# First branch's projection of two token blocks moved into and behind the last attention head; w_out loaded by column halves

## The chip, the cores and the metric

One core of one Trainium2 chip runs the kernel. Its engines work beside each other, each on its own list of instructions in a fixed order: TensorE (PE, matrix multiplications and transposes; PEld is its weight load), VectorE (DVE), ScalarE (ACT), GpSimd (POOL) and SyncE (SP, which here issues most loads and stores; POOL and ACT issue some). The metric is the device time of one execution, in microseconds (us).

## The reference

One layer of a decoder with two token mixers, 2048 tokens, width 1024, all float32:

```python
h = rms_norm(x, norm_mix)
q, c_kv, k_rope, q_idx, k_idx, w_idx, uv, gates = split(h @ w_in)
y_a = dsa_mixer(...)                  # 8 heads; 256 keys per query, chosen by an indexer
y_b = chunked_gmlp(uv, ...)           # u * (W_s LN(v) + b), chunks of 128
g_a, g_b = split(sigmoid(gates))
merged = g_a * (y_a @ w_proj_a) + g_b * (y_b @ w_proj_b)
x = x + merged @ w_out
h = rms_norm(x, norm_ffn)
x = x + (silu(h @ w_gate) * (h @ w_up)) @ w_down
return rms_norm(x, final_norm)
```

The change touches the line `merged` and the load of `w_out`. `y_a` and `y_b` are 2048 x 512, both projections 512 x 1024.

## The kernel before, in words

A float32 product is made of three passes: every operand is split into a part h that the fast float format holds and a remainder l (`split`, L148 to L157: a copy, then a subtraction), and `mm3` (L159 to L163) adds h·h, h·l and l·h. So one 512-token column block of a projection with 4 weight tiles is 12 matrix instructions.

The work runs in stages: input projections and the choice of keys; attention over 8 heads (L901 to L937); the merge and `w_out` with the residual (called stage 3 here, L940 to L1112); the two feed-forward products by a seven-product scheme; the down projection and the final norm.

**Attention.** For head h and each of four blocks j of 512 queries, `s_stage` makes scores (PE), adds the mask (DVE, tile Pt, L818) and takes exponentials (ACT, L824); `v_stage` transposes the probabilities (tile ptp, L835), splits them (pth, ptl) and multiplies by the values (tile O, L842 and L843), and at its end turns the result (pto, L855) and stores it to `d_ya` (L859). A loop over the 32 blocks interleaves `v_stage` of a block with `s_stage` of the next. Into every block it also puts some units of a filler generator, as many as the table `FILL` says for j = 0 to 3. The filler is `project_b`: for each 512 tokens, four units that turn 128 columns of `y_b` (`branch_T`, tile pty, four transposes each) and eight units that project (`project`, tile ppr, 12 matrix instructions, L161 to L163), multiply by the gate (DVE, tile sg, L887) and store to `d_mb`. That is 48 units, 6 for each of the 8 heads.

**Stage 3.** For each j of four 512-token blocks: `y_a` of the block is turned (`a_T`), then for m = 0 to 7 the projection of `y_a` is made (`project`), added to `d_mb` (POOL, tile mb, L1072) and split (mgh, mgl); then for m = 0 to 7 the product with `w_out` (tile po, 24 matrix instructions, all eight mgh and mgl as operands), the residual and the squares. At j = 0 the sixteen half rows of `w_out` are loaded and split in the same loop over m (tile wor, L1082, into woh and wol). The block before's norm is finished by `stats` (pss, pbc) and, from j = 2 on, `prep_b` readies the next stage's operands. `branch_T` and `project` have in stage 3 a pool of their own (`pr`) with 4 buffers for loads, 4 for sg and 3 for each half of a split weight; in attention the pool `fill` has 2 of each.

**What sets the order.** The kernel is written once as a sequence and a scheduler puts it into each engine's list; a buffer that is used again waits for its last reader. SP's list is in order too: a load that waits for a buffer holds back all behind it. On-chip memory is given out as a stack from the left and one from the right; a tile of stage 3 waits for the attention tile that lies at its address.

Of the kernel before, what the change touches and what calls it, by code (L numbers as in the profile page):

```python
# [11 lines left out]
F32 = mybir.dt.float32  # L12
F32R = mybir.dt.float32r
# [4 lines left out]
ALU = mybir.AluOpType  # L18
# [3 lines left out]
P = 128  # L22
S = 2048
# [3 lines left out]
H = 8  # L27
# [12 lines left out]

FILL = (1, 1, 2, 2)

# [17 lines left out]
def block_kernel(ctx, tc, xT, xN, pos, g_mix, w_in, g_kv, w_ukT, w_uvT, ln_g, ln_b, w_sT, b_sT,  # L60
# [704 lines left out]


    c2 = ExitStack()
    mp, _ = open_pool("mp", stack=c2)
    aw, _ = open_pool("aw", 2, stack=c2)
    fl_, _ = open_pool("fill", stack=c2)  # L770
    masks = []
# [89 lines left out]

    def branch_T(pl, src, j, tag, bk, nb):

        yh = pl.tile([P, 4, 512], F32R, name="yth", tag="yh" + tag, bufs=1)
        yl = pl.tile([P, 4, 512], F32R, name="ytl", tag="yl" + tag, bufs=1)
        for c in range(4):
            yt = pl.tile([P, 4, P], F32, name="ytk", tag="fin", bufs=nb)
            sp.dma_start(yt, src[j * 512:(j + 1) * 512, c * P:(c + 1) * P].rearrange("(t p) c -> p t c", p=P))
            pt = bank(bk, "pty")
            for t in range(4):  # L870
                pe.transpose(pt[:, t * P:(t + 1) * P], yt[:, t], ident)
            split(yh[:, c, :], yl[:, c, :], pt, dve)
            yield yh, yl

    def project(pl, w_p, m, y, s, rows, bk, nb):

        wh = pl.tile([P, 4, P], F32R, name="wph", tag="wph", bufs=2 + nb // 4)
        wl = pl.tile([P, 4, P], F32R, name="wpl", tag="wpl", bufs=2 + nb // 4)
        raw = pl.tile([P, 4, P], F32, name="wpr", tag="fin", bufs=nb)
        sp.dma_start(raw, w_p[m])  # L880
        split(wh, wl, raw, pool, hi=pool)
        pm = bank(bk, "ppr")
        for k in range(4):
            mm3(pm, wh[:, k, :], wl[:, k, :], y[0][:, k, :], y[1][:, k, :], k == 0, k == 3)
        sg = pl.tile([P, 512], F32, name="sg", tag="sg", bufs=nb)
        sp.dma_start(sg, d_sg[s * D + m * P:s * D + (m + 1) * P, rows])
        dve.scalar_tensor_tensor(sg, sg, 1.0, pm, op0=ALU.add, op1=ALU.mult)  # L887
        return sg

    def project_b():  # L890

        for j in range(4):
            rows = slice(j * 512, (j + 1) * 512)
            for yb in branch_T(fl_, d_yb, j, "b", "C", 2):
                yield
            for m in range(KT):
                sg = project(fl_, w_pb, m, yb, 1, rows, "C", 2)
                pool.dma_start(d_mb[m * P:(m + 1) * P, rows], sg)
                yield

    def interleave(gens):  # L901
# [19 lines left out]
    for n, (h, j) in enumerate(blocks):  # L921
# [137 lines left out]
    sp.dma_start(gf, g_ffn)  # L1059
    sp.dma_start(gl, g_fin)  # L1060
    for j in range(4):
        rows = slice(j * 512, (j + 1) * 512)
        if j == 0:
            ya = a_T(0)
        mh, ml = [], []
        for m in range(KT):
            mb = pw.tile([P, 512], F32, name="mb", tag="mb", bufs=4)
            sp.dma_start(mb, d_mb[m * P:(m + 1) * P, rows])
            sg = project(pr_, w_pa, m, ya, 0, rows, "A", 4)
            if after and m == 1:  # L1070
# [7 lines left out]
            if j == 0:
                for n in range(2):
                    ns = slice(n * 512, (n + 1) * 512)  # L1080
                    raw = pw.tile([P, 512], F32, name="wor", tag="xo", bufs=4)
                    sp.dma_start(raw, w_out[m * P:(m + 1) * P, ns])  # L1082
                    split(woh[m][:, ns], wol[m][:, ns], raw, dve, 0.5)
# [287 lines left out]
```

## Time and profile before

| what | value |
|---|---|
| time, median of 3 runs (lowest to highest) | 3208.24 us (3203.16 to 3210.06) |
| the profiled execution's own time | 3207.25 us |
| its span in the trace | 3205.5 us |
| PE busy | 3061.6 us, 96% |
| DVE, ACT, POOL busy | 71%, 45%, 39% |
| attention's last instruction on PE (last pto) | 1598.5 us after the start |

In the trace's rows an instruction is given with its line, engine, operation and tiles (out<-in); in brackets stands the engine's idle time just before it and what ended it. "PEclk" is the share of full speed that TensorE's clock was granted, a mean over the stretch: it has two levels, 1.2 and 2.4 GHz (0.5 and 1.0). At 1.0 a 512-column matrix instruction starts every 0.23 us, though its own duration is printed as 0.39.

### The profile page before, as it was taken

What the parts mean: (1) busy time and instruction counts of PE and PEld (TensorE: products, weight loads), DVE (VectorE), ACT (ScalarE), POOL (GpSimd) and SP (SyncE); (2) the same over time, 40 slices, a digit from 0 to 9 for tenths busy, and PEclk for the clock granted to TensorE, in tenths of its full rate; (3) what the DMA queues carried; (4) which work ended last, traced back from release to release, by engine and by line L of the source; (5) the groups of instructions that cost most, each with busy time, mean ns of one, the idle gap of its engine ahead of it and who ended that gap; (6) DMA issues with size and microseconds to landing.
All of it is one profiled execution on the core that took longest, in us unless ns stands there. A gap on an engine that the chain in (4) does not pass through costs nothing.

```text
span 3205.5 us, 43210 instructions
## 1 busy us (share of the span) xinstructions
PE 3061.6 (96%) x14568; PEld 2516.7 (79%) x14568; DVE 2280.2 (71%) x4150; ACT 1435.1 (45%) x2704; POOL 1255.6 (39%) x1218
## 2 busy tenths in 40 slices
PE   7998999998999999999999999999999999999998
PEld 6876777777778788888777777888878888788887
DVE  8369999999751888877754657777887677544565
ACT  6434435453343767767522125333443333333442
POOL 3644333362454323232253423333345555531220
PEclk9999999999999999999999999999999999999999
DMA  6324333332553222222265853444544444754463
GB/s 204 109 73 138 104 100 102 121 109 81 181 185 125 74 74 78 70 88 69 95 223 168 272 180 122 148 142 150 201 174 173 168 170 158 271 182 141 136 193 106
DMA packets 254416, 453.34 MB, mean 141 GB/s; under 512 B 35568, under 2 KB 79088, under 8 KB 254064
## 3 DMA queue, kind: packets, MB, share of 16 engines
q1 hardware_dynamic: 233840, 390.78, 37.2%
q0 software_dynamic: 15744, 51.39, 4.3%
q10 hardware_dynamic: 4608, 8.39, 0.7%
q8 instruction: 114, 1.87, 0.2%
q14 instruction: 110, 0.90, 0.1%
HBM read 299.54 MB, written 150.93 MB: 141 GB/s over the span
## 4 chain that ended last, share of the span: by engine, by line
PE 67%; DVE 17%; DMA 5%; issue 4%; ACT 3%; POOL 1%; SPq 0%; DVEq 0%; ACTq 0%; POOLq 0%
PE pgu L162 8%; PE pgu L161 7%; PE pgu L163 7%; PE pdn L162 4%; PE pdn L161 4%; PE pdn L163 4%; DVE X L489 4%; PE ptp L835 3%; DVE y L532 3%; PE pm L161 2%; PE pm L162 2%; PE pm L163 2%; PE O L842 2%; PE O L843 2%; PE pg L161 1%
## 5 line engine op out<-in xcount | busy, mean ns | idle before, releaser
L975 POOL TENSOR_TENSOR cmb<-fraw 128x512 f32<-128x512 f32 x275 | 396.7, 1448 | 490.4 <-DVE wfl L154 450.0
L161 PE MATMUL pgu<-fh,wfh 128*128 128x512 f32 x1232 | 480.0, 391 | 7.5 <-ACT fh L153 5.8
L162 PE MATMUL pgu<-fl,wfh 128*128 128x512 f32 x1232 | 481.4, 391 | 2.7 <-DVE fl L154 2.7
L163 PE MATMUL pgu<-fh,wfl 128*128 128x512 f32 x1232 | 481.1, 391 | 0.1
L161 PEld LDWEIGHTS pgu<-fh,wfh 128*128 128x128 f32 x1232 | 232.0, 189 | 58.0 <-ACT fh L153 7.0
L162 PEld LDWEIGHTS pgu<-fl,wfh 128*128 128x128 f32 x1232 | 232.5, 189 | 52.1 <-DVE fl L154 4.0
L489 DVE SCALAR_TENSOR_TENSOR X<-rl,wi,X 128x512 f32<-128x512 f32 (+3 forms) x266 | 232.3, 883 | 56.5 <-ACT rl L485 43.4
L163 PEld LDWEIGHTS pgu<-fh,wfl 128*128 128x128 f32 x1232 | 232.4, 189 | 49.5 <-DVE wfl L154 1.3
L153 ACT ACTIVATE wfh<-cmb 128x512 fp32r<-128x512 f32 x220 | 138.5, 630 | 261.1 <-POOL cmb L975 133.1
L162 PE MATMUL pdn<-ua,uw 128*128 128x512 f32 (+1 forms) x660 | 247.6, 376 | 2.2 <-DVE ua L154 2.2
L154 DVE TENSOR_TENSOR wfl<-cmb,wfh 128x512 fp32r<-128x512 f32 x220 | 183.8, 843 | 90.0 <-ACT wfh L153 89.4
L154 DVE TENSOR_TENSOR ua<-raw,ua 128x512 fp32r<-128x512 f32 (+1 forms) x165 | 119.6, 729 | 177.7 <-ACT ua L153 177.7
L163 PE MATMUL pdn<-ua,uw 128*128 128x512 f32 (+1 forms) x660 | 245.3, 375 | 0.0
L161 PE MATMUL pdn<-ua,uw 128*128 128x512 f32 (+1 forms) x660 | 239.7, 376 | 1.7 <-ACT ua L153 1.7
L1151 DVE TENSOR_TENSOR s<-s,pgu 128x512 f32<-128x512 f32 x264 | 174.9, 679 | 86.8 <-PE pgu L163 47.8
L161 PE MATMUL pm<-wh,hT 128*128 128x512 f32 (+1 forms) x576 | 221.8, 389 | 13.6 <-ACT zq L413 4.9
L485 ACT ACTIVATE rl<-sc 128x512 f32<-128x512 f32 (+3 forms) x304 | 158.5, 549 | 155.6 <-DVE X L489 87.9
L162 PE MATMUL pm<-wl,hT 128*128 128x512 f32 (+1 forms) x576 | 222.3, 387 | 0.5 <-POOL wl L154 0.4
L163 PE MATMUL pm<-wh,lT 128*128 128x512 f32 (+1 forms) x576 | 221.6, 385 | 0.0
L153 ACT ACTIVATE pth<-ptp 128x512 fp32r<-128x512 f32 (+1 forms) x320 | 162.3, 531 | 121.1 <-PE ptp L835 112.2
L154 POOL TENSOR_TENSOR uw<-raw,uw 128x512 fp32r<-128x512 f32 x77 | 108.4, 1416 | 260.2 <-ACT uw L153 233.9
L154 DVE TENSOR_TENSOR ptl<-ptp,pth 128x512 fp32r<-128x512 f32 (+1 forms) x320 | 185.8, 605 | 30.5 <-ACT pth L153 28.7
(315 smaller groups left out, 7729.1 us busy)
## 6 DMA issues: line engine op xcount, KB each, us to landing
raw<-d_a SPq DMA_DIRECT2D x143, 256.0 KB, 2.7
wraw<-in_w_in_dram SPq DMA_DIRECT2D x64, 512.0 KB, 4.4
d_a<-cmb SPq DMA_DIRECT2D x110, 256.0 KB, 2.3
fraw<-in_w_gate_dram SPq DMA_DIRECT2D x22, 1024.0 KB, 4.9
fraw<-in_w_up_dram SPq DMA_DIRECT2D x22, 1024.0 KB, 5.1
d_sg<-zg POOLq DMA_DIRECT2D x64, 256.0 KB, 2.6
sg<-d_sg SPq DMA_DIRECT2D x64, 256.0 KB, 3.7
d_w<-cmb SPq DMA_DIRECT2D x55, 256.0 KB, 2.1
```

The costliest lines, as they stand in the source:

```text
L153: act.activation(h, src, AF.Copy)
L154: lo.tensor_tensor(l, src, _f(h), op=ALU.subtract)
L161: pe.matmul(out, ah, bh, start=first, stop=False, skip_group_check=onto)
L162: pe.matmul(out, ah, bl, start=False, stop=False, skip_group_check=onto)
L163: pe.matmul(out, al, bh, start=False, stop=last, skip_group_check=onto)
L485: act.activation(r[:, :w], sc[:, :w], AF.Relu)
L489: dve.scalar_tensor_tensor(xs, r[:, :w], wi[:, i, h:h + 1], xs, op0=ALU.mult, op1=ALU.add)
L532: dve.tensor_scalar(y, Xs[p], t[:, p:p + 1], None, op0=ALU.is_ge, op1=ALU.add, accum_out=c[:, p:p + 1])
L835: pe.transpose(pt[:, t * P:(t + 1) * P], out["P"][t, kt // 8][:, (kt % 8) * P:(kt % 8 + 1) * P], ident)
L842: pe.matmul(O[:, cs], V, a[:, cs], start=(kt == 0), stop=False)
L975: eng.tensor_tensor(s, blocks[form[0]], blocks[form[1]], op=form[2])
L1151: dve.tensor_tensor(s[to], s[to], b, op=op)
```

## The change

Four things are done.

1. `FILL` goes from (1, 1, 2, 2) to (1, 2, 2, 2), so that the 48 units of `project_b` are used up in the first seven heads. In the last head nothing is put into block j = 0; blocks 1, 2 and 3 get four units each of the new generator `project_a(0)`: 4 turning units, then 8 projecting units for the first 512 tokens of `y_a`. A projecting unit loads the tile of `d_mb` too (mba), adds on POOL, and stores the merged tile to the new `d_mg`.
2. `project_a(1)` (the next 512 tokens) is written right behind the attention loop, ahead of stage 3's loop.
3. Stage 3 loads j = 0 and 1 from `d_mg` and has no projection there; j = 2 and 3 are as before.
4. `w_out` is loaded ahead of the loop, first the left 512 columns of all 8 rows, then the right.

The pool `fill` is opened below attention's pools and lives until j = 3; it replaces `pr`. It has 3 buffers for loads, 3 for sg and 2 for each half of a split weight. The number of instructions on PE, DVE and ACT is unchanged; POOL and SP get 16 stores and 16 loads more.

```diff
-FILL = (1, 1, 2, 2)
+FILL = (1, 2, 2, 2)
...
+    d_mg = tc.dram_tile([D, S // 2], F32, name="d_mg")
...
+    fl_, c3r = open_pool("fill")
     c2 = ExitStack()
     mp, _ = open_pool("mp", stack=c2)
     aw, _ = open_pool("aw", 2, stack=c2)
-    fl_, _ = open_pool("fill", stack=c2)
...
-    def branch_T(pl, src, j, tag, bk, nb):
+    def branch_T(src, j):
...
-            yt = pl.tile([P, 4, P], F32, name="ytk", tag="fin", bufs=nb)
+            yt = fl_.tile([P, 4, P], F32, name="ytk", tag="fin", bufs=3)
...
-    def project(pl, w_p, m, y, s, rows, bk, nb):
+    def project(w_p, m, y, s, rows, bk):
 
-        wh = pl.tile([P, 4, P], F32R, name="wph", tag="wph", bufs=2 + nb // 4)
-        wl = pl.tile([P, 4, P], F32R, name="wpl", tag="wpl", bufs=2 + nb // 4)
-        raw = pl.tile([P, 4, P], F32, name="wpr", tag="fin", bufs=nb)
+        wh = fl_.tile([P, 4, P], F32R, name="wph", bufs=2)
+        wl = fl_.tile([P, 4, P], F32R, name="wpl", bufs=2)
+        raw = fl_.tile([P, 4, P], F32, name="wpr", tag="fin", bufs=3)
...
+    def project_a(j):
+
+        rows = slice(j * 512, (j + 1) * 512)
+        for ya in branch_T(d_ya, j):
+            yield
+        for m in range(KT):
+            sg = project(w_pa, m, ya, 0, rows, "C")
+            mb = fl_.tile([P, 512], F32, name="mba", tag="fin", bufs=3)
+            sp.dma_start(mb, d_mb[m * P:(m + 1) * P, rows])
+            pool.tensor_tensor(sg, sg, mb, op=ALU.add)
+            pool.dma_start(d_mg[m * P:(m + 1) * P, rows], sg)
+            yield
...
-        gens.append((islice(fill, FILL[j]), FILL[j]))
+        if h + 1 < H:
+            gens.append((islice(fill, FILL[j]), FILL[j]))
+        elif j:
+            gens.append((islice(fill_a, 4), 4))
...
+    for _ in project_a(1):
+        pass
+    for n in range(2):
+        ns = slice(n * 512, (n + 1) * 512)
+        for k in range(KT):
+            raw = pw.tile([P, 512], F32, name="wor", tag="xo", bufs=4)
+            sp.dma_start(raw, w_out[k * P:(k + 1) * P, ns])
+            split(woh[k][:, ns], wol[k][:, ns], raw, dve, 0.5)
     for j in range(4):
...
-            sp.dma_start(mb, d_mb[m * P:(m + 1) * P, rows])
-            sg = project(pr_, w_pa, m, ya, 0, rows, "A", 4)
+            sp.dma_start(mb, (d_mg if j < 2 else d_mb)[m * P:(m + 1) * P, rows])
+            if j > 1:
+                sg = project(w_pa, m, ya, 0, rows, "A")
+                pool.tensor_tensor(mb, mb, sg, op=ALU.add)
```

How the change moves instructions is shown at three places (in the changed kernel the same statements stand one line lower up to L164 and thereabouts, and some 10 lower in stage 3).

**PE, from the last head's block j = 2 into block j = 3** (S: scores; ptp: turned probabilities; ppr: filler). Before:

```order
L814 MATMUL S<-Kst_9189,qah 128x512
L815 MATMUL S<-Kst_9189,qal 128x512
L855 MATMUL pto<-ident,os 128x128 x4
L814 MATMUL S<-Kst_9189,qah 128x512
L815 MATMUL S<-Kst_9189,qal 128x512
L814 MATMUL S<-Kst_9189,qah 128x512
L815 MATMUL S<-Kst_9189,qal 128x512
L835 MATMUL ptp<-ident,Pt 128x128 x6
L842 MATMUL O<-pth,V 128x512
L161 MATMUL ppr<-yth,wph 128x512
```

The change:

```order
L162 MATMUL ppr<-yth,wph 128x512
L163 MATMUL ppr<-ytl,wph 128x512
L164 MATMUL ppr<-yth,wpl 128x512
L815 MATMUL S<-Kst_9190,qah 128x512
L816 MATMUL S<-Kst_9190,qal 128x512
L815 MATMUL S<-Kst_9190,qah 128x512
L816 MATMUL S<-Kst_9190,qal 128x512
L856 MATMUL pto<-ident,os 128x128 x4
L815 MATMUL S<-Kst_9190,qah 128x512
L816 MATMUL S<-Kst_9190,qal 128x512
L836 MATMUL ptp<-ident,Pt 128x128 x3
```

Before, the two projecting units of block j = 2 lie further ahead; now four lie in the block, the last of them just ahead of the block's last scores, so that PE has 24 matrix instructions more between the block's start and the first ptp of the next.

**PE, the end of attention and the start of stage 3** (pty: turned `y_a`; po: product with `w_out`). Before:

```order
L842 MATMUL O<-pth,V 128x128
L843 MATMUL O<-ptl,V 128x128
L855 MATMUL pto<-ident,os 128x128 x4
L871 MATMUL pty<-ident,ytk 128x128 x16
L161 MATMUL ppr<-yth,wph 128x512
L162 MATMUL ppr<-ytl,wph 128x512
```

The change, there and 24 matrix instructions later:

```order
L843 MATMUL O<-pth,V 128x128
L844 MATMUL O<-ptl,V 128x128
L856 MATMUL pto<-ident,os 128x128 x4
L872 MATMUL pty<-ident,ytk 128x128 x16
L162 MATMUL ppr<-yth,wph 128x512
```

```order
L164 MATMUL ppr<-yth,wpl 128x512
L162 MATMUL po<-mgh,woh_18091 128x512 x3
L163 MATMUL po<-mgl,woh_18091 128x512
L164 MATMUL po<-mgh,wol_18099 128x512
L162 MATMUL po<-mgh,woh_18092 128x512
```

The sixteen transposes still stand behind the last pto. Of the block's eight projections two stand ahead of the first po (four before); the other six now lie among the po of j = 0.

**SP, the loads around the same place** (ytk: `y_a`; wpr: projection weights; sg: gates; mb, mba: merged tiles; wor: `w_out`). Before:

```order
L886 DMA sg<-d_sg 128x512 x3
L1068 DMA mb<-d_mb 128x512
L1082 DMA wor<-in_w_out_dram 128x512 x2
L1068 DMA mb<-d_mb 128x512
L1082 DMA wor<-in_w_out_dram 128x512 x2
L1068 DMA mb<-d_mb 128x512 x2
L868 DMA ytk<-d_ya 128x4x128 x4
L886 DMA sg<-d_sg 128x512 x3
L880 DMA wpr<-in_w_pa_dram 128x512
```

The change:

```order
L869 DMA ytk<-d_ya 128x4x128
L887 DMA sg<-d_sg 128x512
L869 DMA ytk<-d_ya 128x4x128
L881 DMA wpr<-in_w_pa_dram 128x512
L909 DMA mba<-d_mb 128x512
L881 DMA wpr<-in_w_pa_dram 128x512
L1080 DMA wor<-in_w_out_dram 128x512 x4
L1087 DMA mb<-d_mg 128x512 x2
L909 DMA mba<-d_mb 128x512
L1087 DMA mb<-d_mg 128x512
L1080 DMA wor<-in_w_out_dram 128x512
```

Before, four loads of `w_out` stand ahead of `y_a`; now all four loads of `y_a` and two of projection weights stand ahead of the first of `w_out`.

## Rows read from the trace of the kernel before

**Rows 1.** The page: span; part 1, busy us (share) xinstructions.

```profile
span 3205.5 us, 43210 instructions
PE 3061.6 (96%) x14568; PEld 2516.7 (79%) x14568; DVE 2280.2 (71%) x4150; ACT 1435.1 (45%) x2704; POOL 1255.6 (39%) x1218
```

**Rows 2.** Windows: attention; stage 3. Length, PE, PEld, DVE, ACT, POOL, PEclk, DMA.

```profile
1040.00:1565.00 525.00, 508.38 (x2986) 426.99 (x2986) 431.84 (x1064) 373.72 (x774) 172.90 (x212) 0.99 0.23 74
1630.00:1906.00 276.00, 266.34 (x1188) 217.22 (x1187) 142.10 (x207) 55.01 (x92) 108.43 (x91) 0.99 0.63 206
```

**Rows 3.** Timeline of PE: start, us; heads 2, 3 and 7, start of j = 3.

```profile
1224.31 0.55 PE L835 MATMUL ptp<-ident,Pt 128*128 128x128 f32 x3 [1.42 <-ACT Pt L824]
1226.06 0.50 PE L842 MATMUL O<-pth,V 128*128 128x512 f32 x1 [1.21 <-ACT pth L153]
1226.39 0.39 PE L161 MATMUL ppr<-yth,wph 128*128 128x512 f32 x1
1226.62 0.39 PE L162 MATMUL ppr<-ytl,wph 128*128 128x512 f32 x1
...
1296.04 0.50 PE L842 MATMUL O<-pth,V 128*128 128x512 f32 x1 [0.96 <-ACT pth L153]
```

**Rows 4.** Windows around the end of attention, columns as in rows 2.

```profile
1570.00:1585.00 15.00, 11.09 (x45) 8.24 (x44) 7.38 (x20) 6.95 (x13) 1.96 (x3) 0.77 0.04 9
...
1600.00:1615.00 15.00, 10.87 (x35) 7.54 (x36) 11.24 (x13) 6.68 (x11) 9.33 (x9) 0.66 0.92 306
1615.00:1630.00 15.00, 12.42 (x47) 9.72 (x46) 12.74 (x15) 5.58 (x9) 11.04 (x9) 0.89 0.80 263
```

**Rows 5.** Waits of PE from 1565 to 1630: us in total, times, longest.

```profile
PE ptp L835 <- ACT Pt L824: 3.2, 1, 3.2
PE po L161 <- ACT mgh L153: 2.6, 1, 2.6
PE ppr L161 <- POOL wph L150: 2.1, 2, 1.1
PE pty L871 <- DMA ytk<-d_ya: 1.7, 2, 1.5
PE pty L871 <- DVE ytl L154: 1.2, 1, 1.2
PE O L842 <- ACT pth L153: 0.7, 1, 0.7
```

**Rows 6.** Timeline of PE: the last pto; the first po.

```profile
1598.49 0.66 PE L855 MATMUL pto<-ident,os 128*128 128x128 f32 x4 [0.69 <-ACT os L846]
...
1622.11 0.73 PE L161 MATMUL po<-mgh,woh 128*128 128x512 f32 x2 [2.58 <-ACT mgh L153]
```

**Rows 7.** Groups of instructions of DVE and POOL, 1600 to 1660: busy us, mean ns.

```profile
L157 DVE SCALAR_TENSOR_TENSOR wol<-wor,woh 128x512 fp32r<-128x512 f32 x16 | 17.3, 1113 | 3.4 <-ACT woh L156 3.3
...
L887 DVE SCALAR_TENSOR_TENSOR sg<-sg,ppr 128x512 f32<-128x512 f32 x9 | 6.1, 682 | 11.7 <-PE ppr L163 11.6
...
L151 POOL TENSOR_TENSOR wpl<-wpr,wph 128x512 fp32r<-128x512 f32 x11 | 15.7, 1433 | 0.1
L1072 POOL TENSOR_TENSOR mb<-mb,sg 128x512 f32<-128x512 f32 x8 | 12.3, 1532 | 6.7 <-DVE sg L887 4.2 <-issue 2.4
L150 POOL CAST wph<-wpr 128x512 fp32r<-128x512 f32 x12 | 9.6, 802 | 14.7 <-PE ppr L162 7.7 <-DMA wpr<-in_w_pa_dram 6.8
```

**Rows 8.** DMA: first stage-3 issue; wor's KB and landing, 1585 to 1630; d_mb's landing.

```profile
1588.50 0.32 SPq L1068 DMA_DIRECT2D mb<-d_mb  x1
...
wor<-in_w_out_dram SPq DMA_DIRECT2D x16, 256.0 KB, 4.8
...
DMA to landing us min/median/max: 2.7/3.2/8.9
```

**Rows 9.** Waits of PE from 1630 to 1900: us in total, times, longest.

```profile
PE po L162 <- DVE mgl L154: 3.3, 2, 2.6
PE pty L871 <- issue: 1.6, 1, 1.6
```

More of the change, by code (lines that the diff above doesn't have):

```diff
@@ L860, in v_stage @@
         yield
-    def branch_T(pl, src, j, tag, bk, nb):
-        yh = pl.tile([P, 4, 512], F32R, name="yth", tag="yh" + tag, bufs=1)
-        yl = pl.tile([P, 4, 512], F32R, name="ytl", tag="yl" + tag, bufs=1)
+    def branch_T(src, j):
+        yh = fl_.tile([P, 4, 512], F32R, name="yth")
+        yl = fl_.tile([P, 4, 512], F32R, name="ytl")
         for c in range(4):
-            yt = pl.tile([P, 4, P], F32, name="ytk", tag="fin", bufs=nb)
+            yt = fl_.tile([P, 4, P], F32, name="ytk", tag="fin", bufs=3)
             sp.dma_start(yt, src[j * 512:(j + 1) * 512, c * P:(c + 1) * P].rearrange("(t p) c -> p t c", p=P))
-            pt = bank(bk, "pty")
+            pt = bank("C", "pty")
             for t in range(4):
@@ L884, in project @@
             mm3(pm, wh[:, k, :], wl[:, k, :], y[0][:, k, :], y[1][:, k, :], k == 0, k == 3)
-        sg = pl.tile([P, 512], F32, name="sg", tag="sg", bufs=nb)
+        sg = fl_.tile([P, 512], F32, name="sg", bufs=3)
         sp.dma_start(sg, d_sg[s * D + m * P:s * D + (m + 1) * P, rows])
@@ L893, in project_b @@
             rows = slice(j * 512, (j + 1) * 512)
-            for yb in branch_T(fl_, d_yb, j, "b", "C", 2):
+            for yb in branch_T(d_yb, j):
                 yield
             for m in range(KT):
-                sg = project(fl_, w_pb, m, yb, 1, rows, "C", 2)
-                pool.dma_start(d_mb[m * P:(m + 1) * P, rows], sg)
+                pool.dma_start(d_mb[m * P:(m + 1) * P, rows], project(w_pb, m, yb, 1, rows, "C"))
                 yield
+    def project_a(j):
[9 more added lines that the diff above has]
+            yield
     def interleave(gens):
@@ L910, in interleave @@
                 live.remove(e)
-    fill = project_b()
+    fill, fill_a = project_b(), project_a(0)
     blocks = [(h, j) for h in range(H) for j in range(4)]
@@ L931, in block_kernel @@
             gens.append((values(h // 2 + 1), 4))
-        gens.append((islice(fill, FILL[j]), FILL[j]))
+        if h + 1 < H:
+            gens.append((islice(fill, FILL[j]), FILL[j]))
+        elif j:
+            gens.append((islice(fill_a, 4), 4))
         interleave(gens)
-    for _ in fill:
-        pass
     c2r.close()
@@ L944, in block_kernel @@
     c34 = ExitStack()
-    c3, c3r = ExitStack(), ExitStack()
+    c3 = ExitStack()
     fb0 = open_pool("fb0", side="right", stack=c34)[0]
@@ L950, in block_kernel @@
     pp, _ = open_pool("pp", side="right", stack=c3)
-    pr_, _ = open_pool("pr", 2, stack=c3r)
     SA = {1: ((0, 0), (1, 1), ALU.add), 2: ((1, 0), (1, 1), ALU.add), 3: ((0, 0),), 4: ((1, 1),),
@@ L1033, in a_T @@
     def a_T(j):
-        return list(branch_T(pr_, d_ya, j, "a", "C", 4))[-1]
+        return list(branch_T(d_ya, j))[-1]
     c4 = ExitStack()
@@ L1060, in block_kernel @@
     sp.dma_start(gl, g_fin)
+    for _ in project_a(1):
[6 more added lines that the diff above has]
+            split(woh[k][:, ns], wol[k][:, ns], raw, dve, 0.5)
     for j in range(4):
         rows = slice(j * 512, (j + 1) * 512)
-        if j == 0:
-            ya = a_T(0)
         mh, ml = [], []
@@ L1067, in block_kernel @@
             mb = pw.tile([P, 512], F32, name="mb", tag="mb", bufs=4)
-            sp.dma_start(mb, d_mb[m * P:(m + 1) * P, rows])
-            sg = project(pr_, w_pa, m, ya, 0, rows, "A", 4)
+            sp.dma_start(mb, (d_mg if j < 2 else d_mb)[m * P:(m + 1) * P, rows])
+            if j > 1:
+                sg = project(w_pa, m, ya, 0, rows, "A")
+                pool.tensor_tensor(mb, mb, sg, op=ALU.add)
             if after and m == 1:
                 stats(*after, sq3, pw)
-            pool.tensor_tensor(mb, mb, sg, op=ALU.add)
             h = pw.tile([P, 512], F32R, name="mgh", tag="mgh", bufs=8)
@@ L1077, in block_kernel @@
             ml.append(l)
[L1078 to L1083, printed above, removed]
         sa = None
-        if j < 3:
+        if 0 < j < 3:
             ya = a_T(j + 1)
-        else:
+        elif j == 3:
             c3r.close()
```

## The prediction

> **What bounds the kernel now.** The page comes first: PE is busy 3061.6 us of a span of 3205.5 [rows 1]. The next engine, DVE, has 71%. The change leaves PE's 14568 instructions as they are, so it can win only what PE idles or runs at half clock, in the stages that it touches. The windows say how much that is [rows 2]. Attention up to 1565 us has 525.0 − 508.4 = 16.6 us idle at a clock of 0.99; stage 3 from 1630 has 276.0 − 266.3 = 9.7, also at 0.99. Between them lies the dearest piece, and there I read three views.
>
> The windows show the clock [rows 4]: 0.77 over 1570 to 1585, 0.66 over 1600 to 1615, 0.89 up to 1630. There are two levels, so 0.77 is 0.46 × 15 = 6.9 us at 1.2 GHz, and at half speed 6.9 us do 3.4 us of work. PE's waits say what stops it [rows 5]: 3.2 and 0.7 us for ACT at the last head's block j = 3, then 2.6 for mgh, 2.1 for wph, 1.7 for ytk, 1.2 for ytl. The timeline gives the distance [rows 6]: from the last pto (1598.49) to the first po (1622.11) 23.6 us pass, for sixteen transposes (four take 0.66, so 2.6) and four projections (48 × 0.23 = 11.0), with pto itself 14.3 us of work. The other 9.3 are lost.
>
> So the price of the end of attention is 2.6 + 2.1 + 1.7 + 1.2 = 7.6 us of waits, and of clock (0.34 × 15 × 10.87/15) + (0.11 × 15 × 12.42/15) = 3.7 + 1.4 = 5.1, taking busy time alone: 12.7 us. The block before it costs 3.9 + 3.4 = 7.3.
>
> **Part 1, heads 0 to 6.** The start of block j = 3 has a pattern [rows 3]. In four heads (0, 2, 4, 6; head 2 is shown) PE waits 1.42 + 1.21 = 2.63 us, in three (1, 3, 5) about 0.96. The difference is what filled block j = 2: two turning units (8 transposes, about 1.3 us by the 0.66 for four) or two projecting units (24 × 0.23 = 5.5 us). ACT's and DVE's chain for the next scores outlasts PE's block, and a longer block hides more of it. With one unit more in j = 1 the units fall otherwise: by the order j = 2 has two projecting units in four heads, one in one, none in two. I sum 4 × 0.96 + 1.8 + 2 × 2.63 = 10.9 against 4 × 2.63 + 3 × 0.96 = 13.4: 2.5 won. The clock of 0.99 is at most 0.01 × 525 = 5.2 us; the waits shrink by a fifth, so I take a fifth of it, 1.0. **Gain 3.5** (ends: 0, if j = 1 gains nothing and a stall shows elsewhere; 2.5 + 5.2 = 7.7).
>
> **Part 2, the last head.** Block j = 2 now has four projecting units (11 us of PE) where it had two, 5.5 us more against waits of 3.9. What was covered elsewhere loses its cover: j = 0 has no filler (one unit, 2.8 us, less), and j = 1 has four turning units for two projecting ones. The nearest row is a block filled by turning units, 2.63 us with the clock kept. I take it that one such stall appears: 7.3 − 2.6 = **4.7 gained** (ends: 0, the stalls only move; 7.3). The queues: each of these eight projecting units adds an addition on POOL (mba; 1532 ns [rows 7]), a load on SP and a store on POOL. POOL is busy 172.9 of 525 us in attention and DMA 0.23 [rows 2]; eight times (two transfers of 256 KB [rows 8] and 1.5 us) in 40 us is hidden. Without that cover POOL would be late with wph, at the 1.1 us that one such wait costs [rows 5].
>
> **Part 3, the end of attention.** "Over the end of attention" holds for loads and not for PE: the sixteen transposes still stand behind the last pto, and each projection behind them. Won: SP's first load of stage 3, which stood until 1588.5 behind the filler's buffers [rows 8], need not wait, and before the first po there are two projections, not four. New: three load buffers are shared by ytk, wpr and mba. The fourth ytk can issue only when the first has been turned, behind the last pto, and SP's list is in order: behind that load stand wpr, mba and, as the order shows, every load of w_out. A load lands 3.2 us after issue at the median, at least 2.7 [rows 8]. I count 3.2 for the fourth ytk, 0.7 for ytl (of 1.2), 1.0 for wph (one of the two waits), 1.0 for mgh and woh: 5.9, and half of the clock's loss, 2.5: 8.4 us against 12.7. **Gain 4.3** (ends: 7, with the ytk wait gone and the clock as in rows 2; −1, with the waits as long as now and w_out a round of 4.8 us [rows 8] late).
>
> The first po should then come 0.7 + 2.6 + 5.5 + 8 = 17 us behind the last pto. By then, and 5.5 us on, when the eighth row of w_out is wanted, some 5.5 MB must have moved (left half of w_out, d_mg, ytk, weights, gates, mba, stores); at 306 GB/s [rows 4] that is 18 us against 22. It is tight, and the reason for the third rival's weight.
>
> At this place DVE splits w_out with operands both from on-chip memory: wol takes 1113 ns, sg with one operand from PSUM 682 [rows 7], over the same stretch of POOL work. The Trainium skill ("SBUF — State Buffer", § Who interferes with whom) says that a VectorE instruction reading two SBUF operands contends with GpSimd for an exclusive lock. The trace agrees in the direction; it doesn't show that the lock is the cause. Whatever the cause, sixteen such DVE instructions (eight of w_out, eight of mg) now stand close together ahead of the first eight po operands; that they hold po up is the fourth rival.
>
> **Part 4, the rest of stage 3.** Blocks j = 0, 1 lose their projections: the pty wait of 1.6 [rows 9] goes with j = 1's turning. But projections also hid the way from a product to its split. Before j = 2 and j = 3 there stood three and seven of them ahead of the first po, now two and three, with three load buffers for four and two weight buffers for three. Late next is mgl, the wait that is already there (3.3 in two, the longest 2.6 [rows 9]). I add 1.6 of 2.6 at each of the two blocks, 3.2 + 1.0 for wph's wait [rows 5] − 1.6 = **2.6 lost** (ends: 1.6 gained; 2 × 2.6 + 1.0 = 6.2 lost). The 16 stores and 16 loads more (8 MB) meet a DMA share of 0.63 there [rows 2], at 0.23 before; hidden, at 8 MB / 306 GB/s = 27 us of transfer [rows 4] spread over 276 us.
>
> **Sum.** 3.5 + 4.7 + 4.3 − 2.6 = 9.9 from the profiled execution's 3207.25: 3197.3. The median is 1.0 above that execution, so 3198.
>
> **Rivals.**
>
> *All stalls go.* The fill covers the last head, the clock never falls. For: 5.5 us of cover for 3.9. Against: the fourth ytk. With parts 1 to 3 at 7.7, 7.3 and 7 and part 4 as taken: 3208.2 − 19.4 = 3189, less if part 4 gains.
>
> *The change doesn't do what it says* (loads of w_out behind the last transposes). PE stands at the end of attention as it does now, two rounds of four wor buffers landing in 4.8 us each; the gain of part 3 is zero. For: SP's list, four ytk and two wpr ahead of the first wor. Against: eight rows are needed where sixteen half rows were, and in order. 3198 + 4.3 + 1 = 3203.
>
> *Splits slowed beside POOL.* Eight splits of w_out and eight of mg, each 1113 − 682 = 431 ns longer with POOL's additions and splits beside them: 6.9 us, part 3 at −2.6: 3205. For: the two durations. Against: their shapes of work differ otherwise, and the 1113 is in today's time already. The rule of "SBUF — State Buffer" in the Trainium skill would make it this case.
>
> *Slower: the weight ring paces j = 2 and 3.* With two buffers for wph and wpl, weights of unit m + 2 may be split only when ppr of m is done. POOL then has 802 + 1433 ns of split and 1532 of addition [rows 7] per unit, 3.8 us, and load and wait come on top; between them PE has about 30 × 0.23 = 6.9 us of work (a unit and the po among it). It decides when the chain, with a landing of 3.2, passes 6.9: 3.8 + 3.2 = 7.0 stands at the edge if the load isn't ahead. At 1.4 us per unit × 16 units = 22: 3198 + 22 = 3220. For: POOL's 108 us of 276. Against: three buffers let one load run ahead.
>
> **How the numbers follow.** About 0.2%, 6.4 us, is what a measurement of this kernel can tell from no change: faster is below 3201.8, slower above 3214.7. The forecast has 0.54 (its own range 3192 to 3204), all stalls gone 0.12, w_out behind the transposes 0.18, slowed splits 0.08, the ring 0.08. Faster: the forecast but for a tenth (0.49), all of the second, half of the third: 0.70. Slower: the ring and a little: 0.09. Same: 0.21. The range 3185 to 3212 leaves out the ring and part of the ends.
>
> **What would show it.** Heads 0 to 6: 2.63 us at j = 3 in two heads only. Head 7: no wait above 2.7 us at j = 3, clock above 0.9 over its stretch. The end: first po 15 to 19 us behind the last pto, and ytk the largest wait. Stage 3: idle 10 to 15 us over j = 1 to 3, waits for mgl and wph. I am wrong on part 3 if po waits for woh or wol for over 2 us, on part 4 if ppr waits for wph at every unit of j = 2, and on part 2 if a stall of 3 us or a half clock stands at j = 1 of the last head.

## The result and the profile after

The changed kernel takes 3230.78 us (median of 6 runs, 3220.0 to 3237.23) against 3210.1 us before (6 runs): a ratio of 1.0058, 95% interval 1.0044 to 1.0072. A second set of runs gave 3226.18 against 3209.83, 1.0054 (1.0038 to 1.007). Forecast were 3198 us and a range of 3185 to 3212: it is slower, where faster was forecast.

The page of the changed kernel, span and busy times, beside [rows 1]:

```profile
span 3228.2 us, 43312 instructions
PE 3074.5 (95%) x14568; PEld 2529.7 (78%) x14568; DVE 2304.1 (71%) x4150; ACT 1436.1 (44%) x2704; POOL 1258.9 (39%) x1234
```

The same 14568 instructions keep PE busy 12.9 us longer: more of them ran at half clock. The span is 22.7 us longer. The table below is worked out from the first S, the last pto of each head (the last of its four transposes; the timelines begin a group with the first, 0.4 us ahead), and the first and last po on PE in each timeline. "Moved" is the work that the change put there or took away, at 0.23 us for a matrix instruction of a projection (12 x 0.23 = 2.76 for a unit) and 2.6 for sixteen transposes; "lost" is the difference of the lengths less that. Ahead of the first po 24 such instructions stand now. Before, there were 38: three projections and two instructions of the fourth, whose other ten lie behind the first three po. The "four before" of the section on the change, and the 48 of the prediction, count too many.

```
us                     before  changed  moved   lost   changed, 2nd profile   lost
before attention       1028.8   1035.6    0      6.8        1028.6            -0.2
head 0                   80.8     88.7   +2.8    5.1          89.5             5.9
heads 1 to 6            422.4    446.8  +13.8   10.6         445.1             8.9
head 7                   66.8     75.4   +8.1    0.5          75.7             0.8
last pto, first po       23.2     15.8   -3.2   -4.2          17.4            -2.6
first po, last po       278.7    263.1  -21.5    5.9         264.4             7.2
```

The stage before attention has the same instructions in both kernels and scatters by itself (1026 to 1036 us over all profiles here), so its 6.8 us are no part of the cause. Heads 1 to 6, head 0 and stage 3 are. Three places show it.

**The start of block j = 3.** Windows of 12 us from there, heads 0 to 6 in order (length; busy us of PE, PEld, DVE, ACT, POOL; PEclk; DMA share; GB/s). Before:

```profile
1081.00:1093.00 12.00, 9.38 (x41) 7.47 (x41) 5.41 (x10) 5.88 (x12) 5.55 (x7) 0.86 0.22 76
1152.00:1164.00 12.00, 11.05 (x69) 9.18 (x68) 8.57 (x15) 7.13 (x15) 5.33 (x7) 1.00 0.36 119
...
1504.00:1516.00 12.00, 10.05 (x44) 8.04 (x45) 4.97 (x9) 5.19 (x10) 4.76 (x6) 0.86 0.19 64
sum 84.00, PE 72.43 PEld 59.42 DVE 47.94 ACT 42.17 POOL 34.48; mean PE 10.35 PEld 8.49 DVE 6.85 ACT 6.02 POOL 4.93
```

The heads left out stand at 1.00 too. The changed kernel:

```profile
1095.00:1107.00 12.00, 9.80 (x42) 7.65 (x43) 6.26 (x14) 6.13 (x12) 6.98 (x8) 0.86 0.35 120
1170.00:1182.00 12.00, 9.87 (x49) 8.43 (x48) 6.22 (x14) 7.18 (x15) 4.23 (x5) 0.72 0.31 99
1246.00:1258.00 12.00, 10.11 (x44) 8.13 (x45) 6.03 (x10) 5.02 (x10) 6.24 (x8) 0.86 0.39 132
1317.00:1329.00 12.00, 9.26 (x36) 7.33 (x36) 8.76 (x13) 6.17 (x12) 6.53 (x8) 0.66 0.18 56
1399.00:1411.00 12.00, 9.97 (x43) 8.00 (x44) 6.24 (x10) 5.27 (x10) 6.38 (x8) 0.86 0.38 121
1467.00:1479.00 12.00, 10.60 (x57) 8.80 (x57) 7.99 (x12) 5.91 (x11) 3.71 (x5) 0.86 0.16 55
1546.00:1558.00 12.00, 9.87 (x58) 7.97 (x57) 7.76 (x17) 7.52 (x15) 4.62 (x6) 1.00 0.30 100
sum 84.00, PE 69.47 PEld 56.30 DVE 49.27 ACT 43.20 POOL 38.68; mean PE 9.93 PEld 8.04 DVE 7.04 ACT 6.17 POOL 5.53
```

Before, TensorE's clock falls to 1.2 GHz in two of the seven heads, now in six. By (1 − PEclk) × 12 that is 3.4 us of clock before and 14.2 now; PE is busy 3.0 us less as well.

**Head 0, block j = 0.** SP's timeline (start, length, queue, operation). Before:

```profile
973.10 54.07 SPq L774 DMA_DIRECT2D mask<-d_m  x16
1027.26 1.18 SPq L868 DMA_DIRECT2D ytk<-d_yb  x2
```

The changed kernel, SP:

```profile
1033.48 10.03 SPq L775 DMA_DIRECT2D mask<-d_m  x16
1043.55 4.50 SPq L869 DMA_DIRECT2D ytk<-d_yb  x3
```

and its PE:

```profile
1052.98 1.11 PE L872 MATMUL pty<-ident,ytk 128*128 128x128 f32 x4 [3.46 <-DMA ytk<-d_yb]
```

The sixteen mask loads began 55.7 us before the start of attention's first S (1028.8) and now begin 2.1 us before it (1035.6). SP's waits from 1000 to 1050 name what they waited for, a matrix instruction of the stage before:

```profile
SPq L775 <- PE pg L163: 53.6, 1, 53.6
```

The ytk loads stand behind them, and PE waits 3.5 us for the first.

**Head 7 and the end**, PE's timeline, beside [rows 5, 6]:

```profile
1618.04 0.90 PE L836 MATMUL ptp<-ident,Pt 128*128 128x128 f32 x3 [3.27 <-ACT Pt L825]
1619.65 0.79 PE L843 MATMUL O<-pth,V 128*128 128x512 f32 x1 [0.71 <-ACT pth L154]
...
1646.02 0.66 PE L856 MATMUL pto<-ident,os 128*128 128x128 f32 x4 [0.69 <-ACT os L847]
...
1648.53 0.66 PE L872 MATMUL pty<-ident,ytk 128*128 128x128 f32 x4 [0.98 <-DVE ytl L155]
1652.76 1.09 PE L872 MATMUL pty<-ident,ytk 128*128 128x128 f32 x4 [3.58 <-DMA ytk<-d_ya]
1654.43 0.79 PE L162 MATMUL ppr<-yth,wph 128*128 128x512 f32 x1 [0.57 <-POOL wph L151]
...
1662.26 0.96 PE L162 MATMUL po<-mgh,woh 128*128 128x512 f32 x3
```

Head 7's two waits are what they were (3.2 and 0.7 before). The first po stands 16.2 us behind the last pto, where it was 23.6.

### The profile page after: what moved, and what is told of

Same layout as the page of the kernel before. It is cut to its first block, busy times and chain, and to the rows that moved or that the text cites. A ratio compares the mean times of both kernels' runs of the same rounds, so it can differ in the third digit from the quotient of the medians.

```text
span 3228.2 us, 43312 instructions
## 1 busy us (share of the span) xinstructions
PE 3074.5 (95%) x14568; PEld 2529.7 (78%) x14568; DVE 2304.1 (71%) x4150; ACT 1436.1 (44%) x2704; POOL 1258.9 (39%) x1234
## 4 chain that ended last, share of the span: by engine, by line
PE 68%; DVE 17%; DMA 5%; issue 4%; ACT 3%; POOL 1%; SPq 1%; DVEq 0%; ACTq 0%; POOLq 0%
PE pgu L163 7%; PE pgu L162 7%; PE pgu L164 7%; PE pdn L163 4%; PE pdn L164 4%; PE pdn L162 4%; DVE X L490 4%; PE ptp L836 3%; DVE y L533 3%; PE pm L162 2%; PE pm L163 2%; PE pm L164 2%; PE O L843 2%; PE O L844 2%; PE ppr L162 2%
## 5 line engine op out<-in xcount | busy, mean ns | idle before, releaser
L164 PE MATMUL pgu<-fh,wfl 128*128 128x512 f32 x1232 | 481.0, 391 | 0.1
L164 PEld LDWEIGHTS pgu<-fh,wfl 128*128 128x128 f32 x1232 | 232.3, 189 | 49.5 <-DVE wfl L155 1.3
L155 DVE TENSOR_TENSOR wfl<-cmb,wfh 128x512 fp32r<-128x512 f32 x220 | 192.8, 884 | 92.7 <-ACT wfh L154 92.2
L164 PE MATMUL pdn<-ua,uw 128*128 128x512 f32 (+1 forms) x660 | 245.3, 375 | 0.0
L1165 DVE TENSOR_TENSOR s<-s,pgu 128x512 f32<-128x512 f32 x264 | 174.6, 679 | 79.5 <-PE pgu L164 40.5
L164 PE MATMUL pm<-wh,lT 128*128 128x512 f32 (+1 forms) x576 | 223.2, 388 | 0.0
```

The costliest lines, as they stand in the source:

```text
L155: lo.tensor_tensor(l, src, _f(h), op=ALU.subtract)
L164: pe.matmul(out, al, bh, start=False, stop=last, skip_group_check=onto)
L1165: dve.tensor_tensor(s[to], s[to], b, op=op)
```

## Experiments

**e1: the table alone, on the kernel before.**

```diff
-FILL = (1, 1, 2, 2)
+FILL = (1, 2, 2, 2)
```

> The kernel before with FILL (1, 2, 2, 2) and nothing else: the 48 units of project_b are used up in seven heads, the last head has none, project_a stays in stage 3. Theory A (the new table is what loses: the units fall on other places of the blocks, PE still waits over 2 us at the start of block j = 3, and the clock falls there in nearly every head): 3220 to 3232 us, at least four of heads 0 to 6 with a stretch at half clock at the start of j = 3. Rival B (the loss comes from the rest: transfers, the shared load buffers or the place of the pool in memory): 3206 to 3214 us, and at most two such heads.

3214.89 us against 3209.42, ratio 1.0017 (1.0008 to 1.0026): slower, but by 5.5 us, not 11 or more. It lies between the two theories. In this kernel the last head is left empty too, so it isn't the table's price alone. Its profile (that execution took 3223.09 us, 8 above the median) shows theory A's sign: the clock falls at j = 3 in all seven heads, and heads 1 to 6 take 445.0 us, 8.8 lost by the working of the table above, with every pool where it was.

**e2: the changed kernel with the old table.**

```diff
-FILL = (1, 2, 2, 2)
+FILL = (1, 1, 2, 2)
...
-    fill, fill_a = project_b(), project_a(0)
+    fill = chain(project_b(), project_a(0))
...
-        if h + 1 < H:
-            gens.append((islice(fill, FILL[j]), FILL[j]))
-        elif j:
-            gens.append((islice(fill_a, 4), 4))
+        nf = FILL[j] if h + 1 < H else (1, 5, 6, 6)[j]
+        gens.append((islice(fill, nf), nf))
```

> The changed kernel with FILL (1, 1, 2, 2) of before; the last head takes the six units left of project_b and then the twelve of project_a(0), as (1, 5, 6, 6) over j = 0 to 3. Theory A (the table): heads 0 to 6 are as before, 10 to 15 us come back, 3210 to 3219 us or less. Rival B (the rest of the change): 3226 to 3235 us.

3231.11 us, 1.007 (1.0055 to 1.0085): as rival B had it. But eighteen units in the last head make this another kernel: by its profile the last pto to the first po takes 21.7 us, with 10.3 us of waits in it, where the changed kernel has 15.8. Its heads 1 to 6, with the old table, lose 4.2 us where the changed kernel loses 10.6. It couldn't decide, and e6 was made for that.

**e3: w_out's loads alone**, the loop over halves put ahead of stage 3's loop in the kernel before.

> The kernel before with the load and split of w_out ahead of stage 3's loop, left halves first, and nothing else. Theory C (the shorter way from the last pto to the first po comes from moving w_out): the distance falls from 23.6 to under 20 us, time 3203 to 3208 us. Rival D (it comes from the projections that no longer stand there; sixteen loads through four buffers ahead of the loads of y_a hold the transposes back): distance 23 to 32 us, time 3208 to 3220 us.

3208.56 us, 1.0002 (0.9991 to 1.0012), the distance 24.3 us (23.2 before, both counted as in the table): rival D. Loading w_out early shortens nothing by itself; the way to the first po is shorter in the changed kernel, where 24 matrix instructions of projections stand on it, not 38.

**e4: work behind the last scores**, in the kernel before.

```diff
-        gens.append((islice(fill, FILL[j]), FILL[j]))
+        nf = FILL[j]
+        if j == 3:
+            next(fill, None)
+            nf -= 1
+        gens.append((islice(fill, nf), nf))
```

> The kernel before, but at j = 3 the first of the two filler units is issued ahead of the block's own work, so that it stands on PE behind the block's last scores. Theory E (the wait at the start of j = 3 is the way from the last scores over DVE's mask and ACT's exponentials to the first transposed probabilities; only work that stands behind the last scores covers it, however long the block before): PE's waits at j = 3 of heads 0 to 6 fall from 13.4 us to under 7, no half clock there, 3198 to 3206 us. Rival F (the length of the block before decides, as the prediction had it): the waits stay within 1 us a head, 3207 to 3213 us.

3197.84 us against 3209.42, 0.9962 (0.9948 to 0.9976). Its windows at the start of j = 3, heads 0 and 1 and the sum of seven:

```profile
1084.00:1096.00 12.00, 11.53 (x61) 9.21 (x62) 7.15 (x13) 7.09 (x14) 8.14 (x10) 1.00 0.46 148
1152.00:1164.00 12.00, 11.18 (x70) 9.44 (x70) 8.27 (x15) 7.43 (x16) 5.63 (x7) 1.00 0.45 151
...
sum 84.00, PE 79.48 PEld 65.79 DVE 57.11 ACT 46.13 POOL 48.77; mean PE 11.36 PEld 9.40 DVE 8.16 ACT 6.59 POOL 6.97
```

PE is busy 79.5 of 84 us there (72.4 before) and the clock is 1.00 in all seven. No instruction was added; one unit of twelve instructions was moved from somewhere in the block to behind the scores. Theory E holds, and the prediction's reading of [rows 3] falls.

**e6: the changed kernel, heads 0 to 5 with the old table, head 6 with twice as much.**

```diff
-FILL = (1, 2, 2, 2)
+FILL = (1, 1, 2, 2)
...
-            gens.append((islice(fill, FILL[j]), FILL[j]))
+            nf = FILL[j] * (2 if h + 2 == H else 1)
+            gens.append((islice(fill, nf), nf))
```

> The changed kernel with another table: heads 0 to 5 take their six units of project_b as before, (1, 1, 2, 2), head 6 takes twelve, (2, 2, 4, 4), and the last head keeps the twelve of project_a(0). Theory A (the units' places decide heads 1 to 6): the 14 us that heads 1 to 6 lost by the two profiles mostly come back, 3215 to 3222 us. Rival B (with the order of before the clock falls all the same, and the rest lies at head 0 and the last stages): 3225 to 3233 us.

3216.25 us, 9.9 less than the changed kernel measured beside it (3226.18); 1.0021 (1.001 to 1.0031) against before. Theory A. The places of the units in heads 1 to 6 are worth some 10 us. Not all of that is the old places: by the profiles heads 1 to 6 are 11.5 us shorter for their work than in the changed kernel, and 3.0 of these are head 6's, which with its doubled filler idles 0.1 us. The windows at j = 3, heads 1 to 4, show one thing that theory A had not (that execution took 3226.74 us, 10 above the median):

```profile
1166.00:1178.00 12.00, 11.05 (x68) 9.16 (x67) 8.50 (x15) 7.41 (x15) 5.64 (x7) 1.00 0.36 120
1236.00:1248.00 12.00, 9.33 (x33) 6.77 (x32) 4.67 (x10) 5.86 (x12) 4.95 (x8) 0.72 0.16 55
1310.00:1322.00 12.00, 11.04 (x67) 9.09 (x67) 8.36 (x15) 6.98 (x16) 5.12 (x8) 1.00 0.34 116
1379.00:1391.00 12.00, 9.33 (x34) 6.91 (x33) 5.16 (x12) 5.92 (x14) 4.97 (x7) 0.72 0.17 57
```

Heads 2 and 4 have the order and the waits of before (2.64 us, and 2.63 there), and the clock falls there, where it stayed at 1.00 before. Heads 1 and 3, with 0.94 us, stay at 1.00 in both.

**e7: the ytk loads ahead of the masks**, in the changed kernel.

```diff
+    ytk0 = []
+    for c in range(3):
+        yt = fl_.tile([P, 4, P], F32, name="ytk", tag="fin", bufs=3)
+        sp.dma_start(yt, d_yb[0:512, c * P:(c + 1) * P].rearrange("(t p) c -> p t c", p=P))
+        ytk0.append(yt)
     masks = []
...
```

> The changed kernel with the first three loads of ytk issued ahead of the sixteen mask loads. Theory G (the pool fill lies where the masks lay, the masks lie where the stage before still works, so all sixteen wait until its end and hold the ytk loads back on SP; PE waits 3.5 to 4.2 us for the first pty and pays 3.4 us of clock): the wait for ytk in head 0 goes, head 0 takes 81 to 83 us for 88.7, 3222 to 3226 us. Rival H (the masks' late loads themselves hold PE): head 0 within 2 us of 88.7, 3228 to 3233 us.

The wait is gone and head 0 takes 83.5 us for 88.7, close to what theory G said; the time doesn't show it: 3226.63 us, 1.0056 (1.0041 to 1.0072), and 3226.18 for the changed kernel beside it. In that profile stage 3 was 8 to 9 us longer, with a wait of 3.1 us of po at j = 0 and more half clock; why is not known. e14 below tests the masks once more, in e8's order.

**e8: the three together**, with the table of e6, the loads of e7, and the cover of e4 (two units in the last head).

> The changed kernel with three things together: the table of e6, the ytk loads ahead of the masks as in e7, and filler units behind the last scores at j = 3 (one in heads 0 to 6, two in the last). If waits and clock in attention are the whole loss, what is left is the gain at the end of attention and the covered stall of the last head (3.9 us of waits, 3.4 of clock): e4's 3198 less 4 to 10, 3188 to 3195 us. If the longer attention itself costs (12 units more on DVE, ACT and POOL beside it) or stage 3 loses more than 3 us: 3198 to 3212 us.

3195.96 us, 0.9959 (0.9948 to 0.9971), and 3198.34, 0.9965 (0.9951 to 0.9979), in a second set (

> The kernel of e8 once more, beside e14 on the same chip: 3192 to 3200 us, head 0 at 77 to 79 us without a wait for ytk.

). That takes back the whole loss, but beside e4 (3197.84) the change then brings nothing that can be measured. The first of the two times lies between the ranges expected, the second in the slower one.

**e9: the changed kernel again.**

> The changed kernel once more, for a second profile. Theory A: head 0 again 86 to 90 us with the wait for ytk, heads 1 to 6 again at least three stretches at half clock at j = 3; 3226 to 3235 us. Rival (luck of one execution): heads 1 to 6 with at most one such stretch. The stage before attention, whose work is the same in both kernels, is expected between 1027 and 1036 us.

3226.18 us; head 0 89.5 us with a wait of 4.2; the clock at the start of j = 3 in heads 0 to 6 is 0.72, 0.86, 0.86, 0.75, 0.86, 0.86, 1.00. Six of seven again.

**e10: e8 with pools as before**, fill closed with attention and a pool of its own behind it.

```diff
-    fl_, c3r = open_pool("fill")
...
+    fl_, _ = open_pool("fill", stack=c2)
...
+    cur[:] = open_pool("pr", 2, stack=c3r)[0], 4, 3
```

> The kernel of e8, but with the pools of before: fill on top of attention's pools and closed with them (3 load buffers, 3 sg, 2 weight buffers), and a pool of its own for project_a(1) and for j = 2 and 3 (4 load buffers, 4 sg, 3 weight buffers). The masks lie where they lay, so the ytk loads need not go first. Theory I (the three load and two weight buffers cost the 3 us of stage 3 and the wait for the fourth ytk): the longest wait for ytk at the end falls under 2 us and stage 3's idle from 13 to about 10, 3189 to 3194 us. Rival J (what stage 3 lost is that two and three projections stand ahead of po where five and seven stood, and the loads now wait for attention's memory): the waits for mgl at j = 2 and 3 stay, 3194 to 3200 us.

3193.75 us against 3211.22, 0.9949 (0.9933 to 0.9965), the lowest median here. PE's waits in stage 3 (us in total, times, longest), e10 from 1600 to 1885:

```profile
PE po L162 <- ACT woh L157: 4.6, 1, 4.6
PE ppr L162 <- POOL wph L151: 3.5, 2, 2.1
PE po L163 <- DVE mgl L155: 2.6, 1, 2.6
```

and the changed kernel from 1665 to 1930:

```profile
PE po L163 <- DVE mgl L155: 6.9, 4, 2.8
PE po L162 <- ACT mgh L154: 4.4, 3, 1.9
```

Waits for mgl fall from 6.9 to 2.6 us (e8 has 6.9 too) and no po waits longer than 0.8 for mgh, as theory I had it. But the order changed with the pools: 23 matrix instructions of po now stand ahead of the sixteen transposes, the first of them 5.2 us behind the last pto and after the 4.6 us for woh. What the buffers do alone isn't shown. The distance of the medians to e8 (2 to 5 us) lies inside their intervals, so as a time it isn't shown.

**e11: e8 with project_a(0) behind attention.**

```diff
-        elif j:
...
-            gens.append((islice(fill_a, nf), nf))
+    for _ in fill_a:
+        pass
     for _ in project_a(1):
         pass
```

> The kernel of e8, but project_a(0) runs behind attention, ahead of project_a(1); the last head has no filler. Theory K (the twelve units are PE work that costs the same in either place, 24 us; what the last head gains from them is only cover): PE's waits in the last head grow from about 4 to 6 to 12 us, the end of attention is as long plus 24 us, 3198 to 3206 us. Rival L (as additional DVE, POOL and ACT work they hold attention up as much as they cover): within 3 us of e8.

3232.58 us, 1.0065 (1.0051 to 1.0079): 34 to 37 us slower than e8, beyond both theories. PE's waits from 1590 to 1930:

```profile
PE po L162 <- ACT mgh L154: 13.9, 7, 3.8
PE ppr L162 <- POOL wph L151: 8.6, 3, 4.4
```

and POOL's groups from 1592 to 1660, with its idle time ahead of wph; then ACT's timeline:

```profile
L151 POOL CAST wph<-wpr 128x512 fp32r<-128x512 f32 x8 | 6.7, 840 | 14.2 <-DMA wpr<-in_w_pa_dram 13.4 <-PE ppr L164 0.7
```

```profile
1648.75 0.63 ACT L154 ACTIVATE mgh<-mb 128x512 fp32r<-128x512 f32 x1 [8.87 <-DMA mb<-d_mg]
```

Four projections stand ahead of the first po here, and the others lie among the po, much as before. The weights are split late because their loads land late: 13.4 of POOL's 14.2 us of idle time ahead of wph. And mgh waits for merged tiles that are stored to `d_mg` and loaded again. The last head is 21.5 us shorter than in e8 (53.3 for 74.8), and the way from the last pto to the last po 55 us longer (334.0 for 279.0), for 24.7 us of work moved. So the part of the change that moves the first block into the last head is worth much against this order, though not against the order before, where stage 3's tiles take no way over `d_mg`. Which of the two waits costs how much isn't shown.

**e12: e8 with w_out ahead of project_a(1).**

> The kernel of e8 with the loads and splits of w_out ahead of project_a(1). Theory M (SP's list is in order, so loads of w_out behind the waiting fourth ytk are late and po waits for them): the first po comes earlier and no po of j = 0 waits over 1 us, 2 to 4 us faster than e8. Rival N (po waits for mgh and mgl, that is for d_mg, and the transposes now stand behind sixteen loads): the same within 2 us, or up to 6 slower by a longer wait for ytk.

3199.28 us, 0.9961 (0.9948 to 0.9974): the same as e8, rival N's case.

**e14: e8 with the masks first again.**

> The kernel of e8 with the sixteen mask loads ahead of the ytk loads again, as in the changed kernel. Theory G (the displaced masks hold the first filler loads back): head 0 takes 4 to 8 us more than e8's 77.9, with the wait for ytk of 3 us or more, and the time is 3 to 8 us above e8's in the same call. Rival H (e7's time did not fall because the stall in head 0 only takes the place of another wait): within 2 us of e8.

3203.38 us, 0.9979 (0.997 to 0.9988), against 3198.34 for e8 beside it: 5.0 us. Head 0 takes 82.1 us for 77.9, with a wait of 3.8 us for ytk. Theory G, in e8's order; in the changed kernel's own order e7 did not show it.

## Why the prediction was wrong

The loss of 16 to 21 us has one part that the runs show well and one that they show in part. The places of the filler units cost some 10 us (e6; 10.6 and 8.9 by the table above), and 5.5 where the new table stands alone (e1). The displaced masks cost 5 in e8's order (e14), as head 0 does by the table (5.1 and 5.9); but in the changed kernel itself the time did not fall when their wait was gone (e7). With both taken away and the waits at j = 3 covered, nothing is left of the loss beside e4, which has that cover alone (e8). What the change wins at the end of attention (4.2 us, 2.6 in the second profile) it gives back in stage 3 (5.9 and 7.2). In e8 these two rows together are 4.3 us worse than in e4, and head 6, which has twice the filler, is 4.1 us shorter for its work.

- **Part 1 failed, and with the wrong sign.** The step was "a longer block hides more of it". The waits at j = 3 follow the block's last scores, over the mask on DVE and the exponentials on ACT. Work ahead of the scores moves both ends, and only work behind them covers the wait (e4). In the last head, where four projecting units stood ahead, the timelines in the changed kernel show the chain, DVE first:

```profile
1612.25 0.69 DVE L888 SCALAR_TENSOR_TENSOR sg<-sg,ppr 128x512 f32<-128x512 f32 x1 [2.16 <-issue]
...
1615.95 0.75 DVE L819 CUSTOM_DVE_ANT_0 Pt<-S,mask,mn 128x512 f32<-128x512 f32 x1
```

then ACT:

```profile
1616.74 1.15 ACT L825 ACTIVATE Pt<-Pt,mn 128x1024 f32<-128x1024 f32 x1 [4.35 <-DVE mn L819]
...
1617.89 1.13 ACT L825 ACTIVATE Pt<-Pt,mn 128x1024 f32<-128x1024 f32 x1
```

The last mask, the two exponentials behind it, then ptp at 1618.04: ACT had been idle for 4.35 us, waiting for DVE. DVE had stood still for 2.16 us ahead of sg, the gate of the fourth projecting unit, whose last product starts at 1611.77, and made the block's masks behind it. What set odd heads apart from even ones in [rows 3] was not j = 2's filling but the order on PE. In the odd heads of before the second group of three ptp at the start of j = 3 stands ahead of the block's last scores, so only the wait for pth is left; in the even ones it stands behind them (head 2: last scores at 1222.49, ptp at 1224.31). Head 3 before:

```profile
1293.69 0.49 PE L835 MATMUL ptp<-ident,Pt 128*128 128x128 f32 x3
...
1294.68 0.40 PE L815 MATMUL S<-Kst,qal 128*128 128x512 f32 x1
1296.04 0.50 PE L842 MATMUL O<-pth,V 128*128 128x512 f32 x1 [0.96 <-ACT pth L153]
```

In the changed kernel it stands behind them in heads 1, 3 and 5 too. Head 3:

```profile
1318.93 0.40 PE L816 MATMUL S<-Kst,qal 128*128 128x512 f32 x1
1319.87 0.55 PE L836 MATMUL ptp<-ident,Pt 128*128 128x128 f32 x3 [0.54 <-ACT Pt L825]
1321.62 0.79 PE L843 MATMUL O<-pth,V 128*128 128x512 f32 x1 [1.21 <-ACT pth L154]
```

The new table put two projecting units into j = 2 of four heads, and none of them got 0.96 us: they wait 2.1 to 2.3.

- **Part 1's clock.** The text took 1.0 us of gain. Instead half-clock stretches went from two heads to six. The odd heads, whose 0.94 to 0.96 us never brought the clock down (before, e6), got waits of 1.6 to 2.7 us, and it fell in all three in both profiles. Head by head, by the working of the table above, heads 1, 3 and 5 lose 4.0, 7.7 and 3.2 us, and heads 2, 4 and 6 lose −0.2, 0.1 and −4.1. No rival had the odd heads' waits grow and the clock fall there; the nearest one had the clock only getting better.

- **A part that was not in the sum: where the pool lies.** The prediction weighed the pool that moved only by its buffers. Put below attention's pools, it pushes the masks up to places that the stage before still uses (the 53.6 us for pg above; with the pools as before, in e10, the masks begin 56 us ahead of the first S), and SP's order hands the delay on to ytk. The reading of stage 3 (a tile waits for what lies at its address) held at the start of attention as well, and wasn't applied there.

- **Part 2 failed:** 0 gained of 4.7. The last head's waits are 3.3 and 0.7 us, for the reason above. (Before, its j = 1 held one projecting unit, not two as the text has it; no term hangs on that.)

- **Part 3 was right in size, with a wrong count in it.** Forecast were 3.2 us for the fourth ytk, 0.7 for ytl, 1.0 for wph and 1.0 for mgh and woh, 5.9, and the first po 17 us behind the last pto. Measured ahead of the first po: 3.6, 1.0, 0.6 and none, so 5.2 (0.8 for mgh come behind it), and 16.2. Wrong was the work on that way before: 38 matrix instructions of projections, 8.7 us, not 48 and 11.0. So 12.0 of the 23.6 us were work and 11.6 lost, where the prediction has 14.3 and 9.3. The way is 7.4 us shorter with 3.2 us of work less: 4.2 won (2.6 in the second profile), where 4.3 were forecast. Nearly half of it is the clock. The first window below holds 8.6 us of work in 10.7 us of busy time, the first one of before 12.0 in 16.0: 2.1 lost, where it was 4.0. The windows of the changed kernel from the last pto to the first po, and from there to the last:

```profile
1646.00:1662.00 16.00, 10.71 (x43) 8.00 (x44) 6.54 (x9) 5.24 (x9) 5.18 (x6) 0.79 0.71 217
1662.00:1925.00 263.00, 250.26 (x1094) 201.20 (x1093) 152.12 (x210) 59.84 (x100) 97.19 (x85) 0.99 0.71 233
```

The kernel before, the same two:

```profile
1598.50:1622.00 23.50, 16.04 (x58) 11.33 (x58) 18.06 (x20) 11.18 (x19) 13.34 (x12) 0.78 0.90 292
1622.00:1901.00 279.00, 269.24 (x1192) 219.44 (x1193) 146.76 (x212) 55.84 (x94) 114.72 (x95) 0.99 0.64 207
```

- **Part 4 was right in idle time and too small in length.** 263.0 − 250.3 = 12.7 us idle in stage 3 against 279.0 − 269.2 = 9.8 before: 2.9 more, where 2.6 were forecast. By length 5.9 us are lost (7.2 in the second profile). The rest is busy time, 250.3 us where 269.2 − 21.5 = 247.7 would be the same work's; the sum had it at nothing, and its cause is open. mgl waits longest, as named.

- **The rivals.** None had the mechanism that decided. w_out behind the transposes: no po of the changed profile waits for woh or wol. The slowed splits: wol took 872 ns there, where [rows 7] had 1113, and nothing waited for it; mgl took 838, where it had 955 (both over the stretch around the first po). So the case that the prediction drew from the Trainium skill's rule on two SBUF operands ("SBUF — State Buffer", § Who interferes with whom) did not come; whether that rule lengthens these splits no run shows. The weight ring: ppr of j = 2 and 3 doesn't wait for wph in the changed kernel, and in e11 the wait comes from the loads, with 0.7 us for a buffer that ppr still read.

Left open: why the clock stayed at 1.00 in heads 2 and 4 of the kernel before and fell in e6 after the same waits. It stayed at 1.00 in heads 2, 4 and 6 of e3, whose attention is that of before, and fell in all three in e2; e2 and e6 have the moved pool, and whether that has a part in it isn't shown. Head 6 fell before and not in e3, in one order, so a single profile says how often the clock falls only roughly.

## What to carry to other kernels

Ask of a stall where its chain begins: only work that stands behind that point covers it, and moving one unit there in every head (e4) gave 12 us, where four units ahead of it in the last head gave none. Before moving or enlarging a pool, look up what lies at the new addresses and which queue is held up in order. Price a table of placements by the waits that each new place leaves open, the clock included, and not by the amount of work.

## What was not expected of the hardware

In the changed kernel waits that add up to 1.6 to 4.2 us at the start of j = 3, all of them in two or more pieces, came with 1.2 GHz in six of seven heads, in both profiles; single waits of 0.94 to 0.96 us did in none of six heads (before, e6). The stage before attention, the same instructions in all these kernels, took 1026 to 1036 us. In the two profiles of the changed kernel PE is busy there for 954.3 and 954.5 us and idle for 81.2 and 74.2.
